# The second norm's mean taken out ahead of it: w_down's rows centred as they are split, with part of each row's sum on GpSimd

## The chip, the cores and the metric

One Trainium2 chip, one of its cores. The kernel is one launch of one decoder layer; the metric is device time in microseconds (us), the median of the runs shown. The core has five engines that run their own instruction streams and wait for one another by semaphores: TensorE (PE in the profile; PEld is its weight load), VectorE (DVE), ScalarE (ACT), GpSimd (POOL) and SyncE (SP), which here only issues transfers.

## The reference

Float32 throughout, 256 positions, model width D = 1024, one layer. Only the second half touches the change:

```python
x = layer_norm(DEEPNORM_ALPHA * x + mix, ln1_g[l], ln1_b[l])
u = causal_dwconv(x @ w_up[l], conv_w_ffn[l])
f = (jax.nn.silu(u[..., :D_FF]) * u[..., D_FF:]) @ w_down[l]
x = layer_norm(DEEPNORM_ALPHA * x + f, ln2_g[l], ln2_b[l])
```

`layer_norm` takes each row's mean off, divides by the root of the variance plus 1e-5, and applies a factor and an offset per column. D_FF is 2816, so w_down has 22 blocks of 128 rows, each 1024 wide. Ahead of this lie the projections, a causal attention over one block of 256 keys, and a gated convolution.

## The kernel before

**Split products.** TensorE multiplies in a reduced float32 form, so every operand is held as a high part (a copy rounded to that form) and a low part (the rest), and every product is three matmuls: high by high, high by low, low by high (`mm3`, L303). For weights the parts are made on the core: a chunk of two weight units arrives by DMA in a `raw` buffer of 2048 columns (three buffers, issued on SP's queue by `issue_dma`, L169), ScalarE copies it into `wh` (`split_h`, L188) and VectorE subtracts to give `wl` (`split_l`, L194). A unit is 1024 columns on 128 partitions; there are nine buffers for each part. A raw buffer is free again when both parts of its two units are made.

**The feed-forward stage (L849 to L967).** Units of w_up come in pairs, a gate unit `g` and a value unit `v` for each of the 22 blocks of 128 columns. `cols_wide` (L328) and `cols_narrow` (L335) put their products in a pair of PSUM banks `pb`; four small stages (`ffn0` to `ffn3`, L808 to L844) evacuate the pair, run the causal convolution with three taps, multiply by silu, and split the result into f's high and low parts. From the fourth block on a `d` unit, one block of 128 rows of w_down, follows each pair: `down` (L893) multiplies block i of f by it, into four accumulators `d` (two halves t of the positions by two halves of the width). The first 14 blocks of w_down are taken so; the last eight (TAIL) stay for the end, as `t` units.

**The order.** `seq` (L920) lists the units in the order in which TensorE takes them. After the matmuls of entry k, `slot(k, ...)` (L932) emits in this order: ScalarE's part of the FFN stages due, ScalarE's `wh` up to entry k+la+1, VectorE's `wl` up to entry k+la, and VectorE's part of the FFN stages. la is 4, and 5 from k = 20 on. Every engine works its instructions off in this order, so a late one holds up all behind it on that engine.

**The end (`finish`, L970).** For t = 0 the eight tail blocks are multiplied, each followed by its slot; then VectorE adds alpha times the residual `x1` to the accumulators, takes `bn_stats` of each half, combines them (`bn_aggr` in `norm_stats`, L720), GpSimd raises variance + eps to the power -1/2, and VectorE applies factor and offset (`norm_apply`, L727) and stores. For t = 1 the same eight blocks are multiplied for the first half of the width, then for the third and the fourth quarter in banks `e` of their own (`down_part`, L902), so that only the last 256 columns' statistics, the combination and the two passes over the row remain behind the last matmul. The first pass there is `norm_first` (subtract the mean, times the factor; two pieces of 512), the second `norm_second` (times the root, plus the offset; 640 columns, stored on SP's queue, then 384, stored on ScalarE's).

GpSimd does hardly anything in this kernel: constants at the start, the issue of the norm factors' transfers, and four powers on one column.

Of the kernel before, what the change touches and what calls it, by code (L numbers as in the profile page):

```python
# [8 lines left out]
F32 = mybir.dt.float32  # L9
# [3 lines left out]
AF = mybir.ActivationFunctionType  # L13
ALU = mybir.AluOpType

P = 128
S = 256
D = 1024
# [6 lines left out]
NP = DFF // P  # L25
ALPHA = 2.0 ** 0.25
EPS = 1e-5
# [110 lines left out]
def layer_kernel(ctx: ExitStack, tc: tile.TileContext, x, wpack, cpack, ln1_g, ln1_b, ln2_g, ln2_b, out):  # L138
    nc = tc.nc
# [4 lines left out]
    tmp = ctx.enter_context(tc.tile_pool(name="tmp", bufs=1))  # L144
# [42 lines left out]

    def split_h(u):  # L188

        issue_dma(units[u]["chunk"] + RAW_BUFS - 1)  # L190
        alloc(u, "h", "wh")
        nc.scalar.activation(units[u]["h"], raw_of(u), AF.Copy)  # L192

    def split_l(u):  # L194

        alloc(u, "l", "wl")
        nc.vector.tensor_tensor(units[u]["l"], raw_of(u), units[u]["h"].bitcast(F32), op=ALU.subtract)  # L197
# [48 lines left out]
    neghalf = cst.tile([P, 1], F32, name="neghalf")  # L246
# [25 lines left out]
    cs = cst.tile([P, 2, 2, 8], F32, name="cs")  # L272
# [77 lines left out]
    cur = {"u": 0}  # L350
# [309 lines left out]
    for j in range(16):  # L660
        u = U[("g", 0)] + j
# [42 lines left out]
    for half in range(2):  # L704
        for e in range(2):
            ua, uc = U[("ao", half)] + e, U[("co", half)] + e
            for n in range(2):
# [4 lines left out]
                bank = ps_bank(f"y{i}")  # L712
# [7 lines left out]
    def norm_stats(r, stats, pieces):  # L720

        mv = tmp.tile([P, 4], F32, tag="mv", name="mv", bufs=4)
        nc.vector.bn_aggr(mv[:, 0:2], stats[:, 0:pieces, :])
        nc.gpsimd.tensor_tensor(mv[:, 3:4], mv[:, 1:2], neghalf, op=ALU.pow)
        return mv

    def norm_apply(o, r, mv, g, b):  # L727
        nc.vector.scalar_tensor_tensor(o, r, mv[:, 0:1], g, op0=ALU.subtract, op1=ALU.mult)
        nc.vector.scalar_tensor_tensor(o, o, mv[:, 3:4], b, op0=ALU.mult, op1=ALU.add)

    def norm_second(r, mv, ln, cs):
        nc.vector.scalar_tensor_tensor(r[:, cs], r[:, cs], mv[:, 3:4], ln[:, 1, cs], op0=ALU.mult, op1=ALU.add)

    def norm_first(r, mv, ln, cs):
        nc.vector.scalar_tensor_tensor(r[:, cs], r[:, cs], mv[:, 0:1], ln[:, 0, cs], op0=ALU.subtract, op1=ALU.mult)

    x1 = big.tile([P, 2, D], F32, tag="rows", name="x1")
    x1T = big.tile([P, KT, 2, S], F32R, tag="xT", name="x1T")

    def with_eps(stats):  # L740

        nc.vector.tensor_scalar(stats[:, 0, 2:3], stats[:, 0, 2:3], EPS * D, None, op0=ALU.add)

    def residual(t, nh, bank, res, r, stats, piece, c0, c1):
        nc.vector.scalar_tensor_tensor(r[:, c0:c1], res[:, t, c0:c1], ALPHA, bank[:, c0 - nh * 512:c1 - nh * 512],
                                       op0=ALU.mult, op1=ALU.add)
        nc.vector.bn_stats(stats[:, piece, :], r[:, c0:c1])
        if piece == 0:
            with_eps(stats)
# [44 lines left out]
    ln2 = big.tile([P, 2, D], F32, tag="e8", name="ln2")  # L794
# [96 lines left out]
    dacc = [[acc_bank(f"d{t}{nh}") for nh in range(2)] for t in range(2)]  # L891
# [19 lines left out]
    def take(n):  # L911
# [4 lines left out]
                pending.remove((stage, i))  # L916
        return out


    seq = []  # L920
    for c in range(1, NP // 2):
        for e in range(2):
# [8 lines left out]
    done = {"h": cur["u"] - seq[0][2], "l": cur["u"] - seq[0][2]}  # L931
    def slot(k, stages):  # L932


        for st, i in stages:
            FFN[st][0](i)
        la = LA if k < 20 else LA + 1
        while done["h"] < min(len(seq), k + la + 2):
            split_h(seq[done["h"]][2])
            done["h"] += 1  # L940
        while done["l"] < min(len(seq), k + la + 1):
            split_l(seq[done["l"]][2])
            done["l"] += 1
        for st, i in stages:
            FFN[st][1](i)

    tail_from = next(k for k, s in enumerate(seq) if s[0] == "t")
    for k, (kind, i, u) in enumerate(seq[:tail_from]):
        if kind == "g":
            pair, first_unit = ps_pair(f"pb{i}"), u  # L950
            cols_wide(u, pair[:, 0], x1T)
        elif kind == "v":
            cols_wide(u, pair[:, 1], x1T)
            cols_narrow(first_unit, pair[:, 0], x1T)
            cols_narrow(u, pair[:, 1], x1T)
# [11 lines left out]
        slot(k, stages)  # L967


    def finish(t):  # L970
        r = x1[:, t]
        stats = tmp.tile([P, 4, 6], F32, tag="stats", name=f"rstats{t}", bufs=2)
        if t == 0:
            for k in range(TAIL):
                down(NP - TAIL + k, (t,))
                slot(tail_from + k, take(2))
            assert not pending
            for nh in range(2):
                residual(t, nh, dacc[t][nh], x1, r, stats, nh, nh * 512, nh * 512 + 512)
        else:  # L980
            for i in range(NP - TAIL, NP):
                down(i, (t,), (0,))
            nc.vector.scalar_tensor_tensor(r[:, 512:1024], x1[:, t, 512:1024], ALPHA, dacc[t][1], op0=ALU.mult, op1=ALU.add)
            for c in range(2):
                residual(t, 0, dacc[t][0], x1, r, stats, c, c * 256, c * 256 + 256)
            for c in range(2, 4):
                bank = ps_pair(f"e{c}")[:, 0]
                for i in range(NP - TAIL, NP):
                    down_part(i, bank, c)
                nc.vector.tensor_tensor(r[:, c * 256:c * 256 + 256], r[:, c * 256:c * 256 + 256], bank[:, 0:256], op=ALU.add)  # L990
                nc.vector.bn_stats(stats[:, c, :], r[:, c * 256:c * 256 + 256])
        mv = norm_stats(r, stats, 2 if t == 0 else 4)
        if t == 0:
            for c in range(2):
                cc = slice(c * 512, (c + 1) * 512)
                norm_apply(r[:, cc], r[:, cc], mv, ln2[:, 0, cc], ln2[:, 1, cc])
                nc.sync.dma_start(out[0, t * P:(t + 1) * P, cc], r[:, cc])
            return
        for c in range(2):
# [49 lines left out]
```

## Time and profile before

| | us |
|---|---|
| median of 3 runs (367.80 to 368.09) | 367.82 |
| the profiled execution, whole | 367.37 |
| its span, first to last instruction | 365.6 |

The profile is of one execution; its span leaves out 1.77 us that lie around the instructions. In the views a row of instructions gives the start (timeline) or the count, the busy time and the mean of one (groups), then the idle time of the engine just ahead of it and, behind an arrow, what ended that idle time. "L197" is line 197 of the kernel. Consecutive VectorE instructions overlap in the records by about 0.07 us, so starts, not durations, add up.

### The profile page before, as it was taken

Reading aid. Unit: us, or ns where it says so; the run is one execution under the profiler, and the core shown is the slowest. Engines: PE = TensorE matmul, PEld = TensorE weight load, DVE = VectorE, ACT = ScalarE, POOL = GpSimd, SP = SyncE. Lnnn points to the kernel's source line nnn. Section 1 sums busy time; section 2 is a strip of 40 time slices with the busy share of each in tenths; the row PEclk is TensorE's granted clock in tenths of the full one; section 3 lists DMA queues with packets and bytes.
Section 4 is the critical chain, followed back from the end, with each engine's and each line's share of the span. In section 5 each row is a group of like instructions: output and inputs, shape, how many; then the busy total and the mean of one; then the engine's idle time right before and its main releaser. Section 6 shows DMA issues by size and latency. Waiting matters only on the chain.

```text
span 365.6 us, 5334 instructions
## 1 busy us (share of the span) xinstructions
PE 356.8 (98%) x2022; PEld 311.5 (85%) x2022; DVE 295.4 (81%) x510; ACT 217.8 (60%) x372; POOL 7.5 (2%) x26
## 2 busy tenths in 40 slices
PE   8999999999999999999999999999999999999991
PEld 7888888898898999988888888888888888888891
DVE  4696988779986669869769888987879796999784
ACT  4685678576977644633367676675657565676300
POOL 2000000000000000102100000000000000000000
PEclk9999999999999999999999999999999999999998
DMA  7979564336554635487160845439173645562011
GB/s 280 340 291 346 183 231 180 115 125 222 229 196 150 230 117 186 173 331 263 83 230 16 332 141 203 187 160 333 42 316 118 228 151 205 220 238 108 0 59 57
DMA packets 11241, 69.63 MB, mean 190 GB/s; under 512 B 1232, under 2 KB 1616, under 8 KB 4176
## 3 DMA queue, kind: packets, MB, share of 16 engines
q1 hardware_dynamic: 10496, 67.00, 49.4%
q0 software_dynamic: 576, 2.10, 1.7%
q8 instruction: 16, 0.26, 0.3%
q10 hardware_dynamic: 144, 0.20, 0.1%
q14 instruction: 9, 0.07, 0.1%
HBM read 68.24 MB, written 1.05 MB: 190 GB/s over the span
## 4 chain that ended last, share of the span: by engine, by line
PE 98%; DVE 1%; DVEq 0%; issue 0%
PE pb L333 20%; PE pb L340 10%; PE g L333 8%; PE d L305 5%; PE d L306 5%; PE d L307 5%; PE g L340 4%; PE q L558 3%; PE v L558 3%; PE k L558 3%; PE b L333 2%; PE y L326 2%; PE y L325 2%; PE y L324 2%; PE c L333 2%; PE o L307 2%
## 5 line engine op out<-in xcount | busy, mean ns | idle before, releaser
L197 DVE TENSOR_TENSOR wl<-raw,wh 128x1024 fp32r<-128x1024 f32 x90 | 109.9, 1222 | 22.9 <-ACT wh L192 22.4
L192 ACT ACTIVATE wh<-raw 128x1024 fp32r<-128x1024 f32 x90 | 94.6, 1056 | 20.8 <-DMA raw<-in_wpack 20.8
L333 PE MATMUL pb<-x1T,wh 128*128 128x512 f32 x320 | 76.2, 390 | 0.0
L333 PEld LDWEIGHTS pb<-x1T,wh 128*128 128x128 f32 x320 | 59.7, 188 | 12.1
L220 DVE TENSOR_TENSOR wl<-raw,wh 128x1024 fp32r<-128x1024 f32 (+1 forms) x38 | 38.0, 1038 | 6.8 <-ACT wh L219 6.6
L340 PEld LDWEIGHTS pb<-x1T,wl 128*128 128x128 f32 x320 | 41.0, 191 | 1.6
L340 PE MATMUL pb<-x1T,wl 128*128 128x256 f32 x320 | 41.5, 283 | 0.0
L219 ACT ACTIVATE wh<-raw 128x1024 fp32r<-128x1024 f32 (+1 forms) x38 | 32.9, 904 | 13.5 <-DMA raw<-in_wpack 7.8
L333 PE MATMUL g<-xT,wh 128*128 128x512 f32 x128 | 31.7, 394 | 0.0
L305 PE MATMUL d<-wh,f 128*128 128x512 f32 x80 | 31.3, 391 | 0.0
L306 PE MATMUL d<-wl,f 128*128 128x512 f32 x80 | 31.3, 391 | 0.0
L307 PE MATMUL d<-wh,f 128*128 128x512 f32 x80 | 31.1, 389 | 0.0
L333 PEld LDWEIGHTS g<-xT,wh 128*128 128x128 f32 x128 | 23.2, 189 | 4.4
L810 ACT ACTIVATE fb<-pb 128x512 f32<-128x512 f32 x20 | 11.9, 597 | 24.9 <-PE pb L340 24.9
L828 DVE SCALAR_TENSOR_TENSOR fc<-fb,consts,fc 128x254 f32<-128x254 f32 x40 | 19.3, 483 | 1.4
L826 DVE SCALAR_TENSOR_TENSOR fc<-fb,consts,fc 128x255 f32<-128x255 f32 x40 | 19.1, 478 | 0.0
L820 ACT ACTIVATE fc<-fb,consts 128x256 f32<-128x256 f32 x40 | 18.0, 497 | 0.4 <-DVE fb L814 0.2
L307 PEld LDWEIGHTS d<-wh,f 128*128 128x128 f32 x80 | 15.0, 188 | 3.2
L305 PEld LDWEIGHTS d<-wh,f 128*128 128x128 f32 x80 | 15.1, 189 | 2.7
L306 PEld LDWEIGHTS d<-wl,f 128*128 128x128 f32 x80 | 15.1, 188 | 2.6
L340 PEld LDWEIGHTS g<-xT,wl 128*128 128x128 f32 x128 | 16.4, 191 | 0.6
L814 DVE TENSOR_TENSOR fb<-pb,fb 128x512 f32<-128x512 f32 x20 | 13.8, 688 | 3.9 <-ACT fb L810 3.6
(183 smaller groups left out, 607.5 us busy)
## 6 DMA issues: line engine op xcount, KB each, us to landing
raw<-in_wpack SPq DMA_DIRECT2D x55, 1024.0 KB, 4.9
raw<-in_wpack SPq DMA_DIRECT2D x6, 896.0 KB, 5.7
xr<-in_x SPq DMA_DIRECT2D x1, 1024.0 KB, 7.5
ln<-in_ln_g POOLq DMA_DIRECT2D x2, 512.0 KB, 5.6
ln<-in_ln_b POOLq DMA_DIRECT2D x2, 512.0 KB, 6.2
raw<-in_wpack SPq DMA_DIRECT2D x3, 256.0 KB, 3.0
raw<-in_wpack SPq DMA_DIRECT2D x1, 512.0 KB, 5.4
out<-x SPq DMA_DIRECT2D x2, 256.0 KB, 2.9
```

What stands on the lines that cost most here:

```text
L192: nc.scalar.activation(units[u]["h"], raw_of(u), AF.Copy)
L197: nc.vector.tensor_tensor(units[u]["l"], raw_of(u), units[u]["h"].bitcast(F32), op=ALU.subtract)
L219: nc.scalar.activation(h, src, AF.Copy)
L220: (eng or nc.vector).tensor_tensor(l, src, h.bitcast(F32), op=ALU.subtract)
L305: nc.tensor.matmul(o, ah, bh, start=start, stop=False)
L306: nc.tensor.matmul(o, ah, bl, start=False, stop=False)
L307: nc.tensor.matmul(o, al, bh, start=False, stop=stop)
L333: nc.tensor.matmul(bank, un["h"][:, k, :], b[:, k].rearrange("p a s -> p (a s)"), start=k == 0, stop=False)
L340: nc.tensor.matmul(bank[:, 0:S], un["l"][:, k, :], b[:, k, 0], start=False, stop=k == nk - 1)
L558: nc.tensor.matmul(banks[m][t], (xl if p == 2 else xh)[:, k, t * P:(t + 1) * P], wl if p == 1 else wh, start=k == 0 and p == 0, stop=k == ...
L826: nc.vector.scalar_tensor_tensor(c[:, 1:S], pb[:, a * S:a * S + S - 1], w_ffn(1, j), c[:, 1:S], op0=ALU.mult, op1=ALU.add)
L828: nc.vector.scalar_tensor_tensor(c[:, 2:S], pb[:, a * S:a * S + S - 2], w_ffn(0, j), c[:, 2:S], op0=ALU.mult, op1=ALU.add)
```

## The change

A row's mean over the columns of `alpha * x1 + f @ w_down` is the mean of `alpha * x1` plus the mean of `f @ w_down`, and the latter is nothing if each row of w_down has had its own mean taken off first. The change does this:

- **Row sums.** For each of the 22 w_down units (`CENTRED`), `halve` has GpSimd add columns 0 to 511 to columns 512 to 1023 of the raw unit, and then the two halves of the result: 512 and 256 additions per partition. The last 256 are left in `rest`.
- **The split.** In `split_h` ScalarE makes one pass over `rest` with scale -1/D and its accumulator, which gives minus the row's mean in `m` [128, 1], and then makes `wh` with function Identity and bias `m` in place of a plain Copy. In `split_l` VectorE makes `wl` as (raw + m) - wh with scalar_tensor_tensor in place of raw - wh. Other units are split as before.
- **Order.** In `slot`, ahead of each `split_h`, `halve` is called for the entries of `seq` up to two beyond the one to be split.
- **The residual.** After entries 14 and 17 `centred(t)` has ScalarE multiply row half t of x1 by alpha in place with an accumulator, and a small instruction turns the sum into minus its mean, `XM[t]`.
- **The end.** `add_residual` adds accumulator, `XM[t]` and x1 in one instruction. `squares` takes the place of `bn_stats`: one tensor_tensor_reduce per piece, whose accumulator carries the variance from piece to piece, starting from eps. `times_factors` multiplies a piece by the norm's factor as soon as its squares are taken. `bn_aggr` and the addition of eps go; the power is taken of the last accumulator; `store` applies root and offset. For t = 1, behind the last matmul, there remain the last piece's addition, its squares, the power beside its factors, and the two stores.

```diff
+    CENTRED = {U[("dn", d)] + e for d in range(NP // 2) for e in range(2)}
+    def halve(u):
+        raw = raw_of(u)[:, 0]
+        t = tmp.tile([P, 768], F32, tag="pr", name=f"ws{u}", bufs=2)
+        nc.gpsimd.tensor_tensor(t[:, 0:512], raw[:, 0:512], raw[:, 512:1024], op=ALU.add)
+        nc.gpsimd.tensor_tensor(t[:, 512:768], t[:, 0:256], t[:, 256:512], op=ALU.add)
+        units[u]["rest"] = t[:, 512:768]
...
-        nc.scalar.activation(units[u]["h"], raw_of(u), AF.Copy)
+        h, raw = units[u]["h"], raw_of(u)
+        if u in CENTRED:
+            m = tmp.tile([P, 1], F32, tag="wm", name=f"wm{u}", bufs=8)
+            rest = units[u]["rest"]
+            nc.scalar.activation(rest, rest, AF.Copy, scale=-1.0 / D, accum_out=m)
+            units[u]["m"] = m
+            nc.scalar.activation(h, raw, AF.Identity, bias=m)
+        else:
+            nc.scalar.activation(h, raw, AF.Copy)
...
+        if u in CENTRED:
+            nc.vector.scalar_tensor_tensor(units[u]["l"], raw_of(u), units[u]["m"], units[u]["h"].bitcast(F32),
+                                           op0=ALU.add, op1=ALU.subtract)
...
+    def centred(t):
+        m = tmp.tile([P, 2], F32, tag="xm", name=f"xm{t}", bufs=2)
+        nc.scalar.activation(x1[:, t], x1[:, t], AF.Copy, scale=ALPHA, accum_out=m[:, 0:1])
+        nc.scalar.activation(m[:, 1:2], m[:, 0:1], AF.Copy, scale=-1.0 / D)
+        XM[t] = m[:, 1:2]
...
         while done["h"] < min(len(seq), k + la + 2):
+            for j in range(done["m"], min(len(seq), done["h"] + 3)):
+                if seq[j][2] in CENTRED:
+                    halve(seq[j][2])
+                done["m"] = j + 1
             split_h(seq[done["h"]][2])
...
+    def add_residual(t, cc, bank):
+        nc.vector.scalar_tensor_tensor(x1[:, t, cc], bank, XM[t], x1[:, t, cc], op0=ALU.add, op1=ALU.add)
+    def squares(t, cc, var, c):
+        r = x1[:, t, cc]
+        n = cc.stop - cc.start
+        nc.vector.tensor_tensor_reduce(out=scratch([P, n], f"sq{t}{c}"), in0=r, in1=r, scale=1.0 / D,
+                                       scalar=var[:, c - 1:c] if c else EPS, op0=ALU.mult, op1=ALU.add,
+                                       accum_out=var[:, c:c + 1])
+    def times_factors(t, cc):
+        nc.vector.scalar_tensor_tensor(x1[:, t, cc], x1[:, t, cc], 1.0, ln2[:, 0, cc], op0=ALU.mult, op1=ALU.mult)
+    def store(t, cc, rstd, queue):
+        r = x1[:, t, cc]
+        nc.vector.scalar_tensor_tensor(r, r, rstd, ln2[:, 1, cc], op0=ALU.mult, op1=ALU.add)
+        queue.dma_start(out[0, t * P:(t + 1) * P, cc], r)
...
-                nc.vector.bn_stats(stats[:, c, :], r[:, c * 256:c * 256 + 256])
-        mv = norm_stats(r, stats, 2 if t == 0 else 4)
+                squares(t, cc, var, c - 1)
+                if c == 2:
+                    times_factors(t, cc)
+        last = 1 if t == 0 else 2
+        nc.gpsimd.tensor_tensor(var[:, 3:4], var[:, last:last + 1], neghalf, op=ALU.pow)
+        rstd = var[:, 3:4]
...
-        for c in range(2):
-            norm_first(r, mv, ln2, slice(c * 512, c * 512 + 512))
-        for cc, queue in ((slice(0, 640), nc.sync), (slice(640, D), nc.scalar)):
-            norm_second(r, mv, ln2, cc)
-            queue.dma_start(out[0, t * P:(t + 1) * P, cc], r[:, cc])
+            times_factors(t, slice(768, D))
+            store(t, slice(0, 640), rstd, nc.sync)
+            store(t, slice(640, D), rstd, nc.scalar)
```

More of the change, by code (lines that the diff above doesn't have):

```diff
@@ L191, in split_h @@
         alloc(u, "h", "wh")
-        nc.scalar.activation(units[u]["h"], raw_of(u), AF.Copy)
+        h, raw = units[u]["h"], raw_of(u)
[7 more added lines that the diff above has]
+            nc.scalar.activation(h, raw, AF.Copy)
     def split_l(u):
         alloc(u, "l", "wl")
-        nc.vector.tensor_tensor(units[u]["l"], raw_of(u), units[u]["h"].bitcast(F32), op=ALU.subtract)
+        if u in CENTRED:
+            nc.vector.scalar_tensor_tensor(units[u]["l"], raw_of(u), units[u]["m"], units[u]["h"].bitcast(F32),
+                                           op0=ALU.add, op1=ALU.subtract)
+        else:
+            nc.vector.tensor_tensor(units[u]["l"], raw_of(u), units[u]["h"].bitcast(F32), op=ALU.subtract)
     def raw_of(u):
@@ L729, in norm_apply @@
         nc.vector.scalar_tensor_tensor(o, o, mv[:, 3:4], b, op0=ALU.mult, op1=ALU.add)
[L731 to L735, printed above, removed]
     x1 = big.tile([P, 2, D], F32, tag="rows", name="x1")
@@ L917, in take @@
         return out
+    XM = {}
+    def centred(t):
[3 more added lines that the diff above has]
+        XM[t] = m[:, 1:2]
     seq = []
@@ L930, in layer_kernel @@
         seq.append(("t", d, U[("dn", d // 2)] + d % 2))
-    done = {"h": cur["u"] - seq[0][2], "l": cur["u"] - seq[0][2]}
+    done = {"h": cur["u"] - seq[0][2], "l": cur["u"] - seq[0][2], "m": 0}
     def slot(k, stages):
@@ L967, in layer_kernel @@
         slot(k, stages)
+        if k in (14, 17):
+            centred((k - 14) // 3)
+    def add_residual(t, cc, bank):
[12 more added lines that the diff above has]
+        queue.dma_start(out[0, t * P:(t + 1) * P, cc], r)
     def finish(t):
-        r = x1[:, t]
-        stats = tmp.tile([P, 4, 6], F32, tag="stats", name=f"rstats{t}", bufs=2)
+        var = tmp.tile([P, 4], F32, tag="var", name=f"var{t}", bufs=2)
+        halves = (slice(0, 512), slice(512, 1024))
         if t == 0:
@@ L977, in finish @@
             assert not pending
-            for nh in range(2):
-                residual(t, nh, dacc[t][nh], x1, r, stats, nh, nh * 512, nh * 512 + 512)
+            for c, cc in enumerate(halves):
+                add_residual(t, cc, dacc[t][c])
+                squares(t, cc, var, c)
+                times_factors(t, cc)
         else:
@@ L982, in finish @@
                 down(i, (t,), (0,))
-            nc.vector.scalar_tensor_tensor(r[:, 512:1024], x1[:, t, 512:1024], ALPHA, dacc[t][1], op0=ALU.mult, op1=ALU.add)
-            for c in range(2):
-                residual(t, 0, dacc[t][0], x1, r, stats, c, c * 256, c * 256 + 256)
+            add_residual(t, halves[1], dacc[t][1])
+            add_residual(t, halves[0], dacc[t][0])
+            squares(t, halves[0], var, 0)
+            times_factors(t, halves[0])
             for c in range(2, 4):
@@ L989, in finish @@
                     down_part(i, bank, c)
-                nc.vector.tensor_tensor(r[:, c * 256:c * 256 + 256], r[:, c * 256:c * 256 + 256], bank[:, 0:256], op=ALU.add)
-                nc.vector.bn_stats(stats[:, c, :], r[:, c * 256:c * 256 + 256])
-        mv = norm_stats(r, stats, 2 if t == 0 else 4)
-        if t == 0:
[L994 to L999, printed above, removed]
-            norm_first(r, mv, ln2, slice(c * 512, c * 512 + 512))
-        for cc, queue in ((slice(0, 640), nc.sync), (slice(640, D), nc.scalar)):
-            norm_second(r, mv, ln2, cc)
-            queue.dma_start(out[0, t * P:(t + 1) * P, cc], r[:, cc])
+                cc = slice(c * 256, c * 256 + 256)
+                nc.vector.tensor_tensor(x1[:, t, cc], x1[:, t, cc], bank[:, 0:256], op=ALU.add)
+                squares(t, cc, var, c - 1)
+                if c == 2:
+                    times_factors(t, cc)
+        last = 1 if t == 0 else 2
+        nc.gpsimd.tensor_tensor(var[:, 3:4], var[:, last:last + 1], neghalf, op=ALU.pow)
+        rstd = var[:, 3:4]
+        if t == 0:
+            for cc in halves:
+                store(t, cc, rstd, nc.sync)
+        else:
+            times_factors(t, slice(768, D))
+            store(t, slice(0, 640), rstd, nc.sync)
+            store(t, slice(640, D), rstd, nc.scalar)
     for t in range(2):
```

## The prediction

> **What bounds the kernel now.** I read the shares of the engines and the chain of waits first, then the load of each engine in the stages that the change touches, then the rows around the end of those stages. The page's engine row and the head of its chain:
>
> ```profile
> PE 356.8 (98%) x2022; PEld 311.5 (85%) x2022; DVE 295.4 (81%) x510; ACT 217.8 (60%) x372; POOL 7.5 (2%) x26
> PE 98%; DVE 1%; DVEq 0%; issue 0%
> ```
>
> TensorE sets the end almost throughout, and the little behind it is VectorE's closing norm. So a shorter closing norm shows in full, and work added ahead of it shows only where it makes TensorE wait. How much room is there? Busy time of the engines in three stretches: eleven rounds of a pair and a `d` unit, the last five pairs without one, and the eight tail blocks of t = 0.
>
> ```profile
> core 0: us, PE busy (x) PEld busy (x) DVE busy (x) ACT busy (x) POOL busy (x), PEclk, DMA share, GB/s
> 208.50:299.65 91.15, 91.15 (x485) 78.90 (x485) 76.62 (x118) 58.35 (x94) 0.00 (x0) 1.00 0.49 185
> 307.94:335.75 27.81, 27.81 (x161) 24.59 (x161) 26.59 (x45) 18.93 (x33) 0.00 (x0) 1.00 0.50 189
> 335.75:346.65 10.90, 10.90 (x49) 9.01 (x49) 8.71 (x14) 5.78 (x10) 0.00 (x0) 1.00 0.00 0
> ```
>
> In the rounds VectorE is idle for 14.53 us of 91.15; in the last five pairs for 1.22 us of 27.81. There it is nearly as full as TensorE. Its rows at the end of that work, and the chain's first matmul of the last tail block:
>
> ```profile
> 342.44 1.22 DVE L197 TENSOR_TENSOR wl<-raw,wh 128x1024 fp32r<-128x1024 f32 x1
> 343.58 0.42 DVE L844 TENSOR_TENSOR f<-ff,f 128x256 fp32r<-128x256 f32 x1
> 346.01 0.69 DVE L745 SCALAR_TENSOR_TENSOR x<-x,d 128x512 f32<-128x512 f32 x1 [2.02 <-PE d L307]
> ```
> ```profile
> 313.48 3.65 PE pb L333 x16
> 345.29 0.23 PE d L305
> ```
>
> VectorE makes the last low part of f by 344.00, and TensorE takes it at 345.29: 1.29 us of slack. Anything that delays VectorE by more than that makes TensorE wait.
>
> **The part removed: the closing norm of t = 1.** VectorE's rows behind the last matmul, and GpSimd's power beside them:
>
> ```profile
> 358.34 0.43 DVE L991 BATCH_NORM_STATS2 rstats<-x 128x6 f32<-128x256 f32 x1
> 358.80 0.26 DVE L723 BATCH_NORM_AGGREGATE mv<-rstats 128x2 f32<-128x24 f32 x1
> 359.10 1.44 DVE L735 SCALAR_TENSOR_TENSOR x<-x,mv,ln 128x512 f32<-128x512 f32 x2
> 360.64 1.42 DVE L732 SCALAR_TENSOR_TENSOR x<-x,mv,ln 128x640 f32<-128x640 f32 x2
> ```
> ```profile
> 359.14 0.55 POOL L724 TENSOR_TENSOR mv<-mv,neghalf 128x1 f32<-128x1 f32 x1 [9.33 <-DVE mv L723]
> ```
>
> From the statistics to the second pass are 2.30 us (358.34 to 360.64). In its place come the squares of 256 columns, then the power beside one piece of factors. These rows, grouped by shape, price them:
>
> ```profile
> L732 DVE SCALAR_TENSOR_TENSOR x<-x,mv,ln 128x640 f32<-128x640 f32 x1 | 0.9, 885 | 0.1
> L729 DVE SCALAR_TENSOR_TENSOR x<-x,mv,ln 128x512 f32<-128x512 f32 x6 | 4.5, 752 | 1.1 <-POOL mv L724 0.9
> L826 DVE SCALAR_TENSOR_TENSOR fc<-fb,consts,fc 128x255 f32<-128x255 f32 x40 | 19.1, 478 | 0.0
> L417 DVE CUSTOM_DVE_ANT_0 sm<-s,mask 128x256 f32<-128x256 f32 x8 | 3.1, 419 | 0.0
> L417 DVE DVE_READ_ACCUMULATOR2_ANT st<- 128x1 f32 x16 | 1.3, 83 | 0.0
> ```
>
> L417 is the same tensor_tensor_reduce: 0.42 + 0.08 = 0.50 us. The power takes 0.55 us if GpSimd comes first, with 0.04 to its start and about as much back: 0.63. If VectorE's piece of factors (0.48, L826's size) comes first, it may hold GpSimd up; the four powers of this trace show both orders, each with the L728 or L735 instruction that runs beside it:
>
> ```profile
> 164.31 0.75 DVE L728 SCALAR_TENSOR_TENSOR x<-xr,mv,ln 128x512 f32<-128x512 f32 x1
> 165.52 0.75 DVE L729 SCALAR_TENSOR_TENSOR x<-x,mv,ln 128x512 f32<-128x512 f32 x1 [0.46 <-POOL mv L724]
> 175.44 0.75 DVE L728 SCALAR_TENSOR_TENSOR x<-xr,mv,ln 128x512 f32<-128x512 f32 x1
> 349.22 0.78 DVE L728 SCALAR_TENSOR_TENSOR x<-x,mv,ln 128x512 f32<-128x512 f32 x1
> ```
> ```profile
> 164.43 1.06 POOL L724 TENSOR_TENSOR mv<-mv,neghalf 128x1 f32<-128x1 f32 x1 [11.72 <-DVE mv L723]
> 175.49 1.13 POOL L724 TENSOR_TENSOR mv<-mv,neghalf 128x1 f32<-128x1 f32 x1 [8.94 <-DVE mv L723]
> 349.26 0.55 POOL L724 TENSOR_TENSOR mv<-mv,neghalf 128x1 f32<-128x1 f32 x1 [172.64 <-DVE mv L723]
> ```
>
> In the first two cases GpSimd's one-column power ends 0.43 us behind the end of VectorE's instruction (165.49 against 165.06, 176.62 against 176.19), and takes twice as long as in the other two. In those it is through ahead of VectorE, and VectorE's instruction takes 0.78 in place of 0.75. So the two engines get in each other's way over SBUF, and whoever comes first goes first. With VectorE first the power returns 0.48 + 0.43 + 0.04 = 0.95 us after the squares. The stretch is then 1.13 to 1.45 us with either order, and the saving 0.85 to 1.17; I take 0.9, since the factors wait for nothing and should start first. For t = 0 the closing norm lies under t = 1's matmuls (346.65 to 357.86), so its shortening is worth nothing.
>
> **The part added to VectorE.** `wl` of a centred unit becomes scalar_tensor_tensor on 1024 columns. 640 against 512 columns is 133 ns for 128, so 1024 cost 885 + 3 x 133 = 1.28 us. The row of today's subtraction, and that of the one frequent instruction that reads PSUM, in the stretch from 307.94 to 346.65:
>
> ```profile
> L197 DVE TENSOR_TENSOR wl<-raw,wh 128x1024 fp32r<-128x1024 f32 x14 | 17.1, 1222 | 0.9 <-ACT wh L192 0.6
> L814 DVE TENSOR_TENSOR fb<-pb,fb 128x512 f32<-128x512 f32 x6 | 4.1, 687 | 0.1
> ```
>
> That is 0.06 us more per unit, 0.5 us for the eight tail units.
>
> **The part added to GpSimd, and what it does to VectorE.** No two-input GpSimd instruction of any width is in the trace. The nearest rows are its memsets:
>
> ```profile
> L239 POOL MEMSET mask<- 128x384 f32 x1 | 0.4, 412 | 0.0
> L226 POOL MEMSET ident<- 128x128 f32 x1 | 0.2, 204 | 0.3 <-POOLq L1039 0.3
> ```
>
> 256 columns more cost 208 ns: 0.81 ns a column for one stream, 0.10 us fixed. Lower bound, one stream's pace: 0.52 + 0.31 = 0.83 us a unit. Upper bound, two streams one after the other and the whole power (0.55) as fixed cost: 1.38 + 0.97 = 2.35. I take two streams with the memset's fixed cost, 0.93 + 0.52 = 1.45 us a unit, being nearest to rows that hold no arithmetic of a power. In itself this would be free, as GpSimd is idle. But nearly all that VectorE does here reads two operands from SBUF, as L728 does; only L814 takes one of them from PSUM. By the powers' rows, each of GpSimd's additions then takes its time out of VectorE, but for what falls in VectorE's idle time or beside L814.
>
> The Trainium skill says so outright: "SBUF — State Buffer", section "Who interferes with whom", has a VectorE instruction with two SBUF inputs contend with GpSimd reads, the one that starts first holding the port for its whole length. The powers' rows agree, though one column is too short to show a long hold by GpSimd. "GPSIMD Engine Reference", section "Performance versus the Vector engine", gives 4497 ns for an add of 2048 columns; by proportion an estimate for 768 is 1.69 us a unit, and the sum below would come out 1.9 us higher.
>
> In the rounds, from 208.50 to 299.65, the row of L814 is
>
> ```profile
> L814 DVE TENSOR_TENSOR fb<-pb,fb 128x512 f32<-128x512 f32 x11 | 7.6, 689 | 3.7 <-ACT fb L810 3.6
> ```
>
> so 14.53 us idle + 7.6 = 22.1 us of cover for eleven `d` units, against 11 x (1.45 + 0.06) = 16.6. It fits, and at the upper bound (26.5) it lacks 4.4, or 5.6 for all 14 units. I take nothing; units are split four or five entries ahead, which evens out single delays.
>
> In the end stage it doesn't fit. `halve` runs up to eight entries ahead of TensorE, four pairs, so the tail's additions start from about 313.5 (the chain's row), when the raw data are there. Demand: 8 x (1.45 + 0.06) = 12.1 us. Cover: VectorE's idle time 1.22 in the pairs; 10.90 - 8.71 - 2.02 = 0.17 in the tail; the slack of 1.29; and four L814, 2.75: together 5.4 us. TensorE therefore waits 12.1 - 5.4 = 6.7 us for the last tail blocks. Bounds: 7.1 - 5.4 = 1.7 and 19.3 - 5.4 = 13.9.
>
> **ScalarE, and the new wait.** `rest` costs a pass of 256 columns with accumulator, the bias pointer a little more:
>
> ```profile
> L820 ACT ACTIVATE fc<-fb,consts 128x256 f32<-128x256 f32 x40 | 18.0, 497 | 0.4 <-DVE fb L814 0.2
> L833 ACT ACTIVATE fs<-fc 128x256 f32<-128x256 f32 x22 | 9.1, 412 | 4.8 <-DVE fc L828 4.5 <-ACT wh L192 0.3
> L428 ACT ACTIVATION_READ_ACCUMULATOR sm<-sm,st 128x1 f32 x16 | 3.0, 187 | 0.0
> L776 ACT ACT_TABLE_LOAD x1 | 1.3, 1283 | 0.0
> ```
>
> 0.41 + 0.19 + 0.09 (L820, which has a pointer, less L833) = 0.69 us a unit, 5.5 for the tail, against 8.9 us idle in the five pairs and 3.0 a round before: hidden, and worth up to 0.69 a unit without that cover. `wh` now waits for GpSimd; behind it on ScalarE stand the evacuations of `pb`, for which VectorE and then TensorE's pair banks wait. As GpSimd is called two entries ahead, I count no extra for this. `centred` adds two passes in the rounds, hidden too. SP's issues stand in the same order; a raw buffer comes free later only where VectorE is late, which is in the sum.
>
> **The rivals.** (A) The additions find their openings, or hold the port so briefly (0.03 us in the 0.78 row) that VectorE loses nothing: then only the closing norm counts, -0.9 us: 366.9. For it: the short hold in both finishing powers. Against: that was one column, and these are 768. (B) The upper bound holds, or GpSimd starves behind a full VectorE and ScalarE's `wh` stands behind it: rounds and tail both stall, 5.6 + 13.9 - 0.9 = +18.6: 386.4. It decides from 22.1 / 11 - 0.06 = 1.95 us a unit on. For it: VectorE leaves no gap in the pairs. (C) Identity isn't in the table set in use beside silu, so that each centred unit loads twice: 0.69 + 2 x 1.28 = 3.25 us a unit; in the rounds 0.27 over the 2.98 idle, 14 times, and in the end stage 26.0 against 14.0: about +15, 382. Against: Copy runs here without a load, and L776's is the last. (D) Stall and saving cancel at the low end: the time stays within 0.2%.
>
> **How the numbers follow.** Against the profiled execution: 367.37 - 0.9 + 6.7 = 373.2; the median of the runs lies 0.45 above it, so 373.6. The forecast's own range: 367.82 + 1.7 - 1.17 = 368.4 to 367.82 + 13.9 - 0.85 = 380.9. Chances: forecast 0.52, A 0.24, B 0.13, C 0.04, D 0.07. A measurement of this kernel tells about 0.2% (0.7 us) from no change; A lies just beyond that, so faster 0.24, same 0.07, slower 0.69. The range reaches down to A and up past the forecast, cutting most of B: 366.6 to 384.
>
> **What would show it.** Right: GpSimd busy some 32 us more; its additions stretched or VectorE's instructions beside them longer than their rows here, most between 313 and 340; TensorE idle ahead of `d` matmuls (L305 to L307's successors) in the last tail blocks of t = 0, ended by VectorE; ahead of that, no idle in the rounds. The power must return 0.6 to 1.0 us after the last squares. Wrong: VectorE's instructions keep their lengths beside GpSimd's (A), TensorE idle already in the rounds or ScalarE waiting long for GpSimd (B), loads on ScalarE (C).

## The result, and the profile after

| | before | after |
|---|---|---|
| median | 367.95 us (6 runs) | 386.81 us (6 runs, 385.24 to 387.38) |
| ratio | | 1.0495, interval 1.0475 to 1.0516 |
| span of the profiled execution | 365.6 us | 385.4 us |

The change makes the kernel 18.9 us slower: the forecast's direction and place, at three times its size, and 2.8 us beyond the top of its range. The engine row and the head of the chain of waits on the page of the changed kernel:

```profile
PE 362.8 (94%) x2022; PEld 313.0 (81%) x2022; DVE 310.9 (81%) x510; ACT 232.6 (60%) x422; POOL 57.5 (15%) x70
PE 43%; DVE 25%; DMA 13%; issue 9%; ACT 4%; POOL 4%; POOLq 0%; DVEq 0%; SPq 0%; ACTq 0%
```

TensorE held 98% of the chain and now holds 43%. VectorE is 25% of it, as expected; that transfers are 13% was not. Where were the 19.8 us of span lost? The same five stretches in both kernels, from the busy time of the engines in windows: the fourteen rounds (from the second pair's first matmul), the last pairs (four, to the first matmul of the last one), the last pair with the tail of t = 0 (to VectorE's first residual), t = 1 (to the last quarter's addition), and the close. First before, then after:

```profile
191.70:307.80 116.10, 116.10 (x619) 100.48 (x618) 97.36 (x152) 74.28 (x120) 0.00 (x0) 1.00 0.51 191
307.80:330.00 22.20, 22.20 (x129) 19.63 (x128) 21.16 (x36) 15.09 (x26) 0.00 (x0) 1.00 0.54 201
330.00:346.00 16.00, 16.00 (x80) 13.57 (x79) 13.64 (x22) 9.76 (x17) 0.00 (x0) 1.00 0.12 51
346.00:357.88 11.88, 11.84 (x75) 10.59 (x74) 9.09 (x19) 0.00 (x0) 0.55 (x1) 1.00 0.13 46
357.88:365.60 7.72, 0.00 (x0) 0.00 (x0) 3.96 (x7) 0.00 (x0) 0.55 (x1) 0.81 0.18 68
```
```profile
192.60:311.90 119.30, 117.28 (x618) 100.33 (x617) 97.79 (x148) 79.97 (x146) 25.32 (x24) 1.00 0.46 169
311.90:340.10 28.20, 23.06 (x129) 19.82 (x128) 23.90 (x35) 18.06 (x31) 6.69 (x5) 1.00 0.56 214
340.10:366.60 26.50, 19.85 (x80) 14.75 (x79) 25.71 (x29) 15.48 (x33) 12.62 (x12) 0.87 0.14 48
366.60:378.54 11.94, 11.90 (x75) 10.60 (x74) 9.73 (x19) 0.00 (x0) 1.05 (x1) 1.00 0.12 45
378.54:385.40 6.86, 0.00 (x0) 0.00 (x0) 2.75 (x6) 0.00 (x0) 0.79 (x1) 0.63 0.20 76
```

The columns are those of the prediction's view: the length of the stretch, then busy time of PE, PEld, DVE, ACT and POOL, the granted clock, the share and rate of DMA. Rounds +3.2, pairs +6.0, tail +10.5, t = 1 nothing, close -0.9; the stretches start 0.9 apart. In the tail VectorE is busy for 25.71 of 26.50 us and is the bound. In the rounds it isn't (97.8 of 119.3), and TensorE still waits.

GpSimd's rows, grouped by shape:

```profile
L194 POOL TENSOR_TENSOR ws<-raw 128x512 f32<-128x512 f32 x22 | 32.2, 1462 | 129.8 <-DMA raw<-in_wpack 92.0 <-ACT wh L210 29.0 <-ACT ws L206 8.8
L195 POOL TENSOR_TENSOR ws<-ws 128x256 f32<-128x256 f32 x22 | 18.1, 822 | 1.7
```

2.28 us a unit, near the prediction's upper bound. These spans hold waiting for VectorE too; GpSimd's busy time grew by 50.0 us (7.5 to 57.5), not by some 32. VectorE's timeline in the tail, and GpSimd's beside it:

```profile
343.68 0.96 DVE L842 SCALAR_TENSOR_TENSOR fc<-fb,consts,fc 128x255 f32<-128x255 f32 x1
344.68 1.40 DVE L844 SCALAR_TENSOR_TENSOR fc<-fb,consts,fc 128x254 f32<-128x254 f32 x1
346.00 0.96 DVE L842 SCALAR_TENSOR_TENSOR fc<-fb,consts,fc 128x255 f32<-128x255 f32 x1
346.99 1.58 DVE L844 SCALAR_TENSOR_TENSOR fc<-fb,consts,fc 128x254 f32<-128x254 f32 x1
```
```profile
344.32 1.48 POOL L194 TENSOR_TENSOR ws<-raw 128x512 f32<-128x512 f32 x1
345.87 0.81 POOL L195 TENSOR_TENSOR ws<-ws 128x256 f32<-128x256 f32 x1
347.00 1.29 POOL L194 TENSOR_TENSOR ws<-raw 128x512 f32<-128x512 f32 x1 [0.32 <-ACT ws L206]
```

VectorE's convolution taps, 0.48 us each before, take 0.96 to 1.58, and they alternate with the additions: the one from 344.68 ends at 346.08, 0.28 after the addition of 512 columns (345.80). The hold that the prediction read from powers on one column is there at full length. The Trainium skill's rule ("SBUF — State Buffer", section "Who interferes with whom") that the later of the two waits for the other's end agrees with these rows. What of the one frequent instruction that reads PSUM (L830)? In experiment e1 below, where it is L820, it runs wholly beside an addition; VectorE's rows, then GpSimd's:

```profile
331.09 0.68 DVE L820 TENSOR_TENSOR fb<-pb,fb 128x512 f32<-128x512 f32 x1
331.69 0.92 DVE L843 TENSOR_TENSOR ff<-fs,fc 128x256 f32<-128x256 f32 x1
```
```profile
330.65 1.68 POOL L194 TENSOR_TENSOR ws<-raw 128x512 f32<-128x512 f32 x1 [4.24 <-DMA raw<-in_wpack]
```

L820 keeps its 0.68, and so it is in all eight places of e1 where it overlaps an addition (0.68 to 0.69); L843 behind it, which reads two operands from SBUF and takes 0.42 us alone, ends 0.28 after the addition (332.61 against 332.33).

The rounds tell another story. Pieces of the chain of waits, in order of time (start, length, what):

```profile
200.78 4.84 DMA raw<-in_wpack
205.76 1.48 POOL ws L194
207.30 0.82 POOL ws L195
208.68 1.16 ACT wh L208
209.87 0.82 DVE wl L216
...
216.63 1.21 DVE wl L216
217.88 4.84 DMA raw<-in_wpack
```

It is a loop: VectorE's low part of the second unit of a `d` chunk (a transfer of two w_down units) frees the raw buffer, the chunk three places on is transferred into it, GpSimd adds, ScalarE makes `wh`, VectorE makes `wl`, and the buffer is free again. One turn takes 17.10 us here (200.78 to 217.88) and 19.55 the next (to 237.43), against two rounds of TensorE's, 16.6 us (116.10 / 7). Three chunks hold six units, and a round takes three, so with three raw buffers the loop has two rounds' time.

The close, VectorE and GpSimd on the timeline:

```profile
379.41 0.08 DVE L1008 DVE_READ_ACCUMULATOR2_ANT var<- 128x1 f32 x1
379.53 0.42 DVE L1013 SCALAR_TENSOR_TENSOR x<-x,ln 128x256 f32<-128x256 f32 x1
379.57 0.79 POOL L1049 TENSOR_TENSOR var<-var,neghalf 128x1 f32<-128x1 f32 x1 [8.15 <-DVE var L1008]
380.39 1.41 DVE L1017 SCALAR_TENSOR_TENSOR x<-x,var,ln 128x640 f32<-128x640 f32 x2 [0.44 <-POOL var L1049]
```

VectorE's piece of factors goes first, the power ends 0.41 behind it, and the second pass starts 0.90 after the last squares (379.49): the prediction's 0.95.

### The profile page after: what moved, and what is told of

Read it like the earlier page. It is cut to its first block, busy times and chain, and to the rows that moved or that the text cites. A ratio compares the mean times of both kernels' runs of the same rounds, so it can differ in the third digit from the quotient of the medians.

```text
span 385.4 us, 5435 instructions
## 1 busy us (share of the span) xinstructions
PE 362.8 (94%) x2022; PEld 313.0 (81%) x2022; DVE 310.9 (81%) x510; ACT 232.6 (60%) x422; POOL 57.5 (15%) x70
## 4 chain that ended last, share of the span: by engine, by line
PE 43%; DVE 25%; DMA 13%; issue 9%; ACT 4%; POOL 4%; POOLq 0%; DVEq 0%; SPq 0%; ACTq 0%
DMA raw<-in_wpack 13%; PE g L355 8%; DVE wl L219 4%; DVE wl L216 4%; PE g L362 4%; DVE fc L842 3%; DVE fc L844 3%; PE q L580 3%; PE k L580 3%; PE v L580 3%; ACT wh L208 2%; PE b L355 2%; PE y L348 2%; PE y L347 2%; PE y L346 2%
## 5 line engine op out<-in xcount | busy, mean ns | idle before, releaser
L219 DVE TENSOR_TENSOR wl<-raw,wh 128x1024 fp32r<-128x1024 f32 x68 | 84.1, 1236 | 11.1 <-ACT wh L210 10.9
L210 ACT ACTIVATE wh<-raw 128x1024 fp32r<-128x1024 f32 x68 | 71.4, 1054 | 9.4 <-DMA raw<-in_wpack 9.4
L194 POOL TENSOR_TENSOR ws<-raw 128x512 f32<-128x512 f32 x22 | 32.2, 1462 | 129.8 <-DMA raw<-in_wpack 92.0
L216 DVE SCALAR_TENSOR_TENSOR wl<-raw,wm,wh 128x1024 fp32r<-128x1024 f32 x22 | 30.2, 1373 | 21.8 <-ACT wh L208 21.7
L328 PE MATMUL d<-wl,f 128*128 128x512 f32 x80 | 33.2, 415 | 8.2 <-DVE wl L216 8.2
L327 PE MATMUL d<-wh,f 128*128 128x512 f32 x80 | 32.3, 404 | 0.2 <-ACT wh L208 0.2
L329 PE MATMUL d<-wh,f 128*128 128x512 f32 x80 | 32.1, 401 | 0.0
L844 DVE SCALAR_TENSOR_TENSOR fc<-fb,consts,fc 128x254 f32<-128x254 f32 x40 | 24.8, 620 | 1.4
L208 ACT ACTIVATE wh<-raw,wm 128x1024 fp32r<-128x1024 f32 x22 | 25.4, 1153 | 0.7
L206 ACT ACTIVATE ws<-ws 128x256 f32<-128x256 f32 x22 | 9.0, 408 | 23.9 <-POOL ws L195 23.9
L842 DVE SCALAR_TENSOR_TENSOR fc<-fb,consts,fc 128x255 f32<-128x255 f32 x40 | 21.6, 540 | 0.0
```

What stands on the lines that cost most here:

```text
L208: nc.scalar.activation(h, raw, AF.Identity, bias=m)
L210: nc.scalar.activation(h, raw, AF.Copy)
L216: nc.vector.scalar_tensor_tensor(units[u]["l"], raw_of(u), units[u]["m"], units[u]["h"].bitcast(F32), op0=ALU.add, op1=ALU.subtract)
L328: nc.tensor.matmul(o, ah, bl, start=False, stop=False)
L842: nc.vector.scalar_tensor_tensor(c[:, 1:S], pb[:, a * S:a * S + S - 1], w_ffn(1, j), c[:, 1:S], op0=ALU.mult, op1=ALU.add)
L844: nc.vector.scalar_tensor_tensor(c[:, 2:S], pb[:, a * S:a * S + S - 2], w_ffn(0, j), c[:, 2:S], op0=ALU.mult, op1=ALU.add)
```

## The experiments

Two theories. **L**: the additions hold VectorE up at SBUF. **W**: the units wait for their sums, and the loop through the raw buffers gets too long. Each experiment is an edit of the changed kernel unless it says otherwise.

**One of them at a time.** e1 keeps the additions and lets nobody use them:

```diff
-        if u in CENTRED:
-            ...
-        else:
-            nc.scalar.activation(h, raw, AF.Copy)
+        nc.scalar.activation(h, raw, AF.Copy)
...
-        if u in CENTRED:
-            nc.vector.scalar_tensor_tensor(units[u]["l"], raw_of(u), units[u]["m"], ...)
-        else:
+        if True:
             nc.vector.tensor_tensor(units[u]["l"], raw_of(u), units[u]["h"].bitcast(F32), op=ALU.subtract)
```

> The changed kernel with GpSimd's additions left in, but their sums unused: wh is the plain copy, wl the plain subtraction, nothing waits for a sum (the output lacks the mean of f @ w_down being taken off). Theory L, the additions hold VectorE up at SBUF: most of the loss stays, 378 to 387 us, with VectorE's two-operand instructions stretched as in the changed kernel. Theory W, the units wait for their sums (transfer, additions, ScalarE, VectorE in one loop through three raw buffers): the loss goes, 366.5 to 369 us.

e2 keeps the wait and takes the reading away:

```diff
-        nc.gpsimd.tensor_tensor(t[:, 0:512], raw[:, 0:512], raw[:, 512:1024], op=ALU.add)
-        nc.gpsimd.tensor_tensor(t[:, 512:768], t[:, 0:256], t[:, 256:512], op=ALU.add)
+        nc.gpsimd.tensor_tensor(t[:, 0:1], raw[:, 0:1], raw[:, 1:2], op=ALU.add)
+        for _ in range(3):
+            nc.gpsimd.memset(t, 0.0)
```

> The changed kernel with each unit's two additions replaced by a one-column addition of the raw unit and three memsets of 768 columns (about 2.2 us together by the memset rows, the additions took 2.28): the split waits for GpSimd as long as before, but GpSimd hardly reads SBUF (the sums are zero, so the mean of f @ w_down stays in the output). Theory L: the loss goes, 367 to 370 us, no stretched VectorE instruction. Theory W: it stays, 378 to 387 us.

e4 has neither (e1 without the call of `halve`), and shows what the new end is worth:

> The changed kernel without any centring of w_down: no additions, plain splits; the new closing norm and the centring of x1 stay (the output lacks the mean of f @ w_down being taken off). What the new end is worth by itself: the closing stretch of the changed kernel is 6.86 us from the last matmul's end against 7.74 before, so 366.9 us, 0.9 below the kernel before; 367.8 if the gain is lost elsewhere.

Measured: e4 367.46 us (0.9963 of before, 0.9947 to 0.998; before's median beside these runs was 368.65); e1 377.89, which is 10.4 over e4; e2 378.31, 10.9 over e4. The changed kernel is 19.4 over e4. Each theory holds about half of it, and neither alone is right; the two add up to 21.3. (Medians of before moved between 367.8 and 368.7 from one set of runs to the next, so differences across sets are good to about 1 us.) The stretches from the rounds to the tail, first of e1, then of e2, in the columns above:

```profile
193.60:309.60 116.00, 116.00 (x618) 100.42 (x617) 104.64 (x149) 75.46 (x123) 33.28 (x24) 1.00 0.50 188
309.60:332.10 22.50, 22.50 (x129) 19.72 (x129) 21.43 (x30) 14.68 (x25) 6.66 (x5) 1.00 0.53 198
332.10:357.80 25.70, 19.80 (x80) 15.00 (x79) 24.90 (x30) 11.97 (x21) 14.60 (x12) 0.87 0.13 47
```
```profile
191.80:311.80 120.00, 117.33 (x619) 100.46 (x618) 93.65 (x148) 79.72 (x146) 29.77 (x48) 1.00 0.45 167
311.80:337.60 25.80, 22.85 (x130) 19.83 (x129) 21.51 (x36) 18.10 (x32) 6.36 (x11) 1.00 0.64 238
337.60:357.30 19.70, 17.48 (x79) 13.27 (x79) 17.34 (x29) 15.55 (x33) 14.77 (x22) 1.00 0.16 62
```

The hold (e1) costs nothing in the rounds, though VectorE is busy 7.3 us longer there than before, 0.3 in the pairs, and 9.7 in the tail. It has one more place, ahead of the rounds: the first two units' additions fall beside the first norm's passes over t = 1, which take 0.75 us in the kernel before. One of these passes in e1, and the addition beside it:

```profile
176.50 1.77 DVE L741 SCALAR_TENSOR_TENSOR x<-x,mv,ln 128x512 f32<-128x512 f32 x1 [0.47 <-POOL mv L736]
```
```profile
176.45 1.27 POOL L194 TENSOR_TENSOR ws<-raw 128x512 f32<-128x512 f32 x1
```

The feed-forward stage's first matmul writes `up`; from there to the start of the rounds it takes 20.4 us in e1, 19.0 in the changed kernel, and 18.3 to 18.4 before, in e2 and in e4. The wait (e2) costs 3.9 in the rounds, 3.6 in the pairs and 3.7 in the tail. VectorE's rows in e2 from 320 us on show that writes alone hold nothing up:

```profile
L217 DVE SCALAR_TENSOR_TENSOR wl<-raw,wm,wh 128x1024 fp32r<-128x1024 f32 x8 | 10.3, 1282 | 1.6 <-ACT wh L209 1.6
L845 DVE SCALAR_TENSOR_TENSOR fc<-fb,consts,fc 128x254 f32<-128x254 f32 x12 | 5.8, 484 | 0.4
```

The memsets took longer together with the gaps between them than reckoned: from e2's chain, three starts 0.80 apart behind 0.5 us, 2.6 to 2.9 us a unit against 2.28. So e2 rather overstates the wait.

**By stage.** e5 centres the 14 units of the rounds only, e7 the eight of the tail only:

```diff
-    CENTRED = {U[("dn", d)] + e for d in range(NP // 2) for e in range(2)}
+    CENTRED = {U[("dn", d)] + e for d in range((NP - TAIL) // 2) for e in range(2)}            # e5
+    CENTRED = {U[("dn", d)] + e for d in range((NP - TAIL) // 2, NP // 2) for e in range(2)}   # e7
```

> The changed kernel with only the 14 w_down units of the rounds centred; the eight tail units are split plainly (the output lacks the centring of those rows). By stages of the traces so far: theory L costs nothing here, theory W some 4 us in the rounds, so 370 to 372.5 us with TensorE's lateness building up before the last five pairs and none in the tail.

> The changed kernel with only the eight tail units centred; the 14 units of the rounds are split plainly (the output lacks the centring of those rows). Theory L: its 10.4 us all stand here, with the waits of theory W in pairs and tail on top, 378 to 384 us, TensorE on time up to the last five pairs. If the rounds' lateness is what makes the tail stall, 370 or less.

Measured: e5 377.73, e7 377.17. e5 was a miss. Its rounds take 3.6 us longer, as foreseen; but the four pairs behind them, which have no additions left, take 25.4 against 22.2, and the tail 17.5 against 16.0. The lateness that VectorE and the transfers pick up in the rounds outlasts them, since VectorE has hardly 1 us of idle time in the pairs in which to catch up (in the kernel before, 22.20 - 21.16). Another 2 us lies ahead of the rounds, as in e1 (20.4 us from the first matmul into `up`). e7's expectation was too high by 0.8 us: rounds and pairs on time (116.0 and 22.2), tail 25.1 us, +9.1. The tail's loss therefore needs no lateness from the rounds. The two experiments together, 9.9 + 9.3 over before, plus 0.9 because both have the new end's gain in them, make 20.1 us; the whole change cost 18.9. That the totals lie so near is in part luck: by stages rounds and tail agree (3.6 against 3.2; 1.5 + 9.1 against 10.5), but the pairs make 3.2 against 6.0, and what lies ahead of the rounds makes up for it.

**What is the wait made of?** e9 is e2 with a fourth raw buffer, made room for by eight buffers a part in place of nine; e10 is its control, the same in e4:

```diff
-    RAW_BUFS, HL_BUFS = 3, 9
+    RAW_BUFS, HL_BUFS = 4, 8
```

> e2_writes_only (GpSimd holds the split up but only writes) with four raw buffers in place of three, and eight buffers in place of nine for each part, to make room. If the rounds' and pairs' loss there (about 7.6 us) comes of the loop raw buffer free, transfer, GpSimd, ScalarE, VectorE, raw buffer free, a fourth buffer gives that loop 5.5 us more and the loss goes: at most 4 us over the control e10 (what e2 loses in the tail). If it comes of ScalarE standing before its wait with the evacuations behind it, it stays: 9 to 11 us over the control.

> The control for e9: e4_new_end_alone (plain splits, new end) with four raw buffers and eight for each part. 366.5 to 368 us, as e4's 367.46, if eight buffers a part are enough; more by whatever the missing ninth costs.

Measured: e9 371.57, e10 370.98. The wait, 10.9 us with three buffers, costs 0.6 with four: it is the loop. With the data there earlier ScalarE no longer waits for GpSimd either (28.4 us of such waits in e2, none listed in e9), so its queue behind that wait isn't priced by itself; it had the loop's lateness for its cause. e9's rounds, pairs and tail take as long as before the change; the tail's wait goes as well:

```profile
197.22:313.26 116.04, 116.04 (x619) 100.41 (x617) 99.94 (x155) 83.61 (x155) 34.40 (x48) 1.00 0.53 191
313.26:335.50 22.24, 22.24 (x130) 19.67 (x128) 19.36 (x32) 15.64 (x30) 11.86 (x18) 1.00 0.50 190
335.50:351.49 15.99, 15.99 (x80) 13.55 (x79) 14.62 (x24) 12.74 (x27) 8.95 (x15) 1.00 0.00 1
```

The control's own 3.5 us over e4 lie ahead of the feed-forward stage (its first pair starts at 190.0, e4's at 186.6): presumably the ninth part buffer was needed there.

**What is the hold's size?** e11 is e1 with the first addition of each unit alone:

```diff
-        nc.gpsimd.tensor_tensor(t[:, 512:768], t[:, 0:256], t[:, 256:512], op=ALU.add)
-        units[u]["rest"] = t[:, 512:768]
+        units[u]["rest"] = t[:, 0:512]
```

> e1_sums_unused with only the first of a unit's two additions (512 columns; 1.27 us where it ran undisturbed in e1, against 1.27 + 0.75 for both). The prediction's sum for the end stage with this price: 8 x 1.27 = 10.2 us of GpSimd less 5.4 of cover, 4.8 us over e4's 367.46, so 372.3 us; with both additions the same sum gives 8 x 2.02 - 5.4 = 10.8, where e1 lost 10.4. If the loss goes by the number of additions, half of it, 372.7, which this run can't tell from it; if any addition at all breaks the tail, 376 or more.

Measured 373.45 (372.51 and 374.38): 6.0 over e4, where the sum says 4.8 and half the loss 5.2. It fits the sum within what two runs can tell. By its trace the tail takes 20.75 us, 4.75 more than before, which is the sum's figure; more than 1 us lies ahead of the rounds (19.6 us from the first matmul into `up`), where the sum has no term. e8 puts the sum to the test in the rounds, with e1's edit, the rounds' units alone, and each unit halved twice:

```diff
                 if seq[j][2] in CENTRED:
                     halve(seq[j][2])
+                    halve(seq[j][2])
```

> As e1_sums_unused (plain splits, nothing waits for a sum), but only for the 14 units of the rounds, and each unit's two additions done twice: about 4.1 us of GpSimd a unit. Theory L with the prediction's cover (VectorE's idle time and the L814 rows, 2.01 us a round): 2.0 us a round too much, 14 times, about 395 us. If GpSimd's reads only hold VectorE up in the tail for another reason, 367 to 368.

Measured 383.68: 16.2 over e4, little more than half of what the sum gave. That the rounds stall from some dose on is shown; the cover there is larger than idle time and L814 rows. Part of it may be that VectorE can run late by several units once before TensorE notices (in the changed kernel VectorE is 11.3 us behind at the end of the rounds, L830 of the fourteenth round at 318.81 against L814's 307.50, where TensorE is 4.1 behind). The rest stays open.

**Without GpSimd.** e3 has ScalarE sum all 1024 columns in a pass of its own; e6 takes the sum from the very pass that makes `wh`, and puts the mean into the low part:

```diff
# e3
-            nc.scalar.activation(rest, rest, AF.Copy, scale=-1.0 / D, accum_out=m)
+            nc.scalar.activation(h, raw, AF.Copy, scale=-1.0 / D, accum_out=m)
...
# e6
-            nc.scalar.activation(rest, rest, AF.Copy, scale=-1.0 / D, accum_out=m)
-            nc.scalar.activation(h, raw, AF.Identity, bias=m)
+            s = tmp.tile([P, 1], F32, tag="ws", name=f"ws{u}", bufs=8)
+            nc.scalar.activation(h, raw, AF.Copy, accum_out=s)
+            nc.scalar.activation(m, s, AF.Copy, scale=-1.0 / D)
```

> The changed kernel without GpSimd: ScalarE sums all 1024 columns in one pass with accumulator (written to wh, then overwritten), 1.06 + 0.19 us in place of 0.41 + 0.19; same output. ScalarE's idle time (2.98 us a round, 8.9 in the last five pairs) should hold it. Theories L and W alike: 366.5 to 368 us; if ScalarE's longer work delays the evacuations of pb, 369 to 375.

> No GpSimd and no wait ahead of wh: ScalarE makes wh as the plain copy of the raw unit, with an accumulator on that very pass, and a one-column instruction turns the sum into minus the mean; VectorE's low part takes the mean in ((raw + m) - wh), so the output is the same up to rounding. Added per unit: 0.19 us accumulator and some 0.2 us on ScalarE, 0.06 us on VectorE. Theories L and W both have no hold here: the new end's gain stays, 366.5 to 367.7 us, below the kernel before. If any added wait of wl for a small ScalarE result costs, 369 and more.

Measured: e3 372.04 (the median of five runs from 370.19 to 373.89; 1.0097 of before, 1.006 to 1.0135), a miss; e6 366.75 (0.9971, 0.9961 to 0.9981). e3's profile is of a sixth run, of 376.08 us, so its stretches overstate the loss; they show where it lies. The rounds take 116.2 us, but the pairs 24.6 and the tail 21.8: ScalarE's timeline has no gap from 328.7 to 352 us, where units at 1.04 + 0.19 + 1.15 us follow one another between the evacuations. Idle time summed over a stretch (8.9 + 5.1 us, against 10.7 of work) was no guarantee of a place for work that comes bunched. e6, whose added work is small, loses nothing anywhere; its stretches, and its new rows from 200 to 350 us:

```profile
192.20:308.20 116.00, 116.00 (x618) 100.43 (x617) 98.35 (x152) 80.55 (x152) 0.00 (x0) 1.00 0.51 191
308.20:330.50 22.30, 22.30 (x130) 19.73 (x129) 20.92 (x35) 15.84 (x32) 0.00 (x0) 1.00 0.54 197
330.50:346.45 15.95, 15.95 (x80) 13.53 (x79) 14.30 (x23) 11.29 (x27) 0.00 (x0) 1.00 0.13 55
```
```profile
L206 ACT ACTIVATION_READ_ACCUMULATOR wh<-raw 128x1 f32 x20 | 3.7, 186 | 0.0
L207 ACT ACTIVATE wm<-ws 128x1 f32<-128x1 f32 x20 | 4.1, 203 | 0.6
L216 DVE SCALAR_TENSOR_TENSOR wl<-raw,wm,wh 128x1024 fp32r<-128x1024 f32 x20 | 25.6, 1282 | 6.2 <-ACT wm L207 6.1
```

TensorE has no idle time in any of the three. This version beats both kernels, the one before by 0.3%: the change's idea was worth about 1 us, and the way it takes its row sums cost twenty times that.

## Why the prediction was wrong in size, step by step

- **What bounds the kernel, and where there is room**: right. The place forecast for the stall, the tail of t = 0 with VectorE as the bound, is where most of the loss stands (+10.5), and e7 shows it by itself.
- **The close, -0.9**: right, in its parts (0.90 for the power's return against 0.95) and in the sum (7.72 to 6.86); e4 shows no loss elsewhere from the new end.
- **scalar_tensor_tensor on 1024 columns, 1.28 us**: right (1282 ns undisturbed in e2 and e6).
- **GpSimd's additions take their time out of VectorE**: right in mechanism; e1 has 10.4 us of it with nobody waiting.
- **"I take two streams with the memset's fixed cost, 0.93 + 0.52 = 1.45 us a unit"**: mis-sized. The shortest spans in the trace are 1.27 and 0.74, 2.01 us. With them the prediction's own sum for the tail is 8 x (2.01 + 0.06) - 5.4 = 11.2 in place of 6.7, where 10.5 was measured. That 10.5 also holds part of the wait; the hold by itself is e1's, which lacks the 0.06: 10.7 by the sum, 9.7 measured. The hold ahead of the rounds, 0.7 us in the changed kernel and 2.0 in e1, has no term in the prediction. The Trainium skill's figure, whose estimate stood beside the sum at 1.69 us a unit, was nearer ("GPSIMD Engine Reference", section "Performance versus the Vector engine"), and still short.
- **"As GpSimd is called two entries ahead, I count no extra for this" and "a raw buffer comes free later only where VectorE is late, which is in the sum"**: the steps that failed, worth half the loss. Being called ahead helps nothing where the raw data have not come: GpSimd stood waiting for transfers for 92.0 us, and the tail's additions, expected from about 313.5, began at 328.84 (in e1 at 321.05). The way from the data's arrival to the buffer's release became longer by the additions and by ScalarE's pass over `rest`, the next transfer into that buffer left later by as much, and one turn of the loop outran two rounds of TensorE. The two chunk periods that three buffers leave a transfer were never put into the sum. e2 shows this cost, 10.9 us, without any hold; in e9 a fourth buffer leaves 0.6 of it.
- **"In the rounds ... I take nothing"**: right for the hold (e1's rounds take 116.0 us), wrong for the whole, and the lateness goes on into the pairs (e5).
- **The rivals**: B named a time, 386.4, that lies on the measured one, and two of its signs came: TensorE was idle in the rounds (2.0 us), and ScalarE waited for GpSimd (23.9 us ahead of L206). But the hit is luck, for its reasons are not those of the runs: it had the upper bound's price stall the rounds and the tail, or GpSimd starve behind a full VectorE. The hold doesn't stall the rounds (e1), the additions there took 2.11 us a unit (25.32 over twelve) against 2.01 undisturbed, so GpSimd did not starve, and the rounds' loss is the loop's. A is refuted by the stretched rows. C did not occur: no table load was added.

What stays open: what ScalarE's waiting queue would cost by itself, how much VectorE can give up in the rounds (e8), and how the 6.0 us in the pairs of the changed kernel divide between the two causes, which there meet (e1 alone 0.3, e2 alone 3.6). That a fourth buffer would leave the changed kernel just the hold's loss wasn't tried.

## What to carry to other kernels

When work is put between a transfer's arrival and the release of its buffer, walk the whole loop, buffer free, transfer, each engine, buffer free, and hold its length against what the number of buffers allows; lookahead in the issue order gives nothing where the data themselves come just in time. GpSimd work that reads SBUF, beside a VectorE that is full of instructions with two operands from SBUF, was VectorE's time here (e1), though GpSimd was idle. Look first for a sum that can be had from a pass that is made anyway: e6's accumulator and the one-column instruction behind it cost 0.19 + 0.20 us a unit where the additions cost 2.

## What the runs showed of the hardware

Two-operand additions on GpSimd took 1.27 us for 512 columns and 0.74 for 256 at the shortest, some 2.1 ns a column above 0.2 us fixed. They stretched VectorE instructions with both tensors in SBUF to two and three times their length (0.48 us to 0.96 and 1.58), and left alone the one that reads PSUM (0.68 in e1); memsets on GpSimd stretched none (1282 and 484 ns in e2).

A longer wait also cost TensorE its clock. Behind the longest one of the tail, matmuls of 512 columns followed one another at 0.43 us where they take 0.23, until the clock came back some 4.5 us later; the window's granted clock is 0.87, in e1's tail too, whose longest wait is 3.19 us, and 1.00 in e2's, whose longest is 0.83. A wait of 2.53 us in the changed kernel's pairs (to 334.41) left the clock at 1.00. The rows of the changed kernel:

```profile
358.72 0.80 PE L328 MATMUL d<-wl,f 128*128 128x512 f32 x1 [4.15 <-DVE wl L216]
359.31 0.63 PE L329 MATMUL d<-wh,f 128*128 128x512 f32 x1
359.74 0.63 PE L327 MATMUL d<-wh,f 128*128 128x512 f32 x1
```

It cost the end little here: TensorE had caught up and waited again, for VectorE's low part, at 364.21.
